# Combining a head pair's attention branches one unit later, with one more result tile

## The chip, the cores and the metric

The kernel runs on one core of a Trainium2 chip. The metric is the device time of one execution in microseconds, the median of several runs. A profiled execution gives, beside its own time, a span (first to last instruction), each engine's instructions with their times, and the clock that was granted to TensorE.

## The reference, cut to what matters

The program is a two-layer decoder trunk over 1024 tokens of width 1024. Layer 0 mixes tokens with a gated MLP and with attention of 8 heads of 64; layer 1 has a gated linear attention; each layer ends in a gated MLP with a convolution. The change lies in the attention of layer 0:

```python
B_BRANCHES = ((128, 1), (512, 4), (2048, 16))
...
    outs, lses = [], []
    for window, dilation in B_BRANCHES:
        o_r, l_r = dilated_branch(qh, kh, vh, window, dilation)
        outs.append(o_r)
        lses.append(l_r)
    wts = jax.nn.softmax(jnp.stack(lses), axis=0)
    o = jnp.einsum('rbhs,rbhsc->bhsc', wts, jnp.stack(outs))
```

Each branch is a causal attention in a sliding window over tokens of a certain stride, normalised by itself; the branches' results are then weighted by a softmax over their log-denominators. The kernel has two passes for this: one over neighbouring tokens (called n) and one over tokens with stride 4 (called d), whose mask and counts take in the third branch.

## The kernel before, in words

The engines are written T (TensorE, PE in the profile), V (VectorE, DVE), A (ScalarE, ACT), G (GpSimd, POOL) and Q (the DMA queue of SyncE, SP). The 1024 tokens are 8 tiles of 128, the 8 heads are 4 pairs.

For each pair p, `project(p)` (L741) goes over the 8 token tiles. `projected(n)` (L752) multiplies the normalised tokens by the pair's weights into a PSUM tile pj (24 matmuls of 384 columns; the tag has two banks), squares q and k on ScalarE, takes 1/rms on GpSimd (rq, L767), and writes the scaled q and k to qn on VectorE (L768). That last instruction is the last reader of pj and frees its bank. ScalarE copies v to vN, and a DMA stores it to vd (L764). Then q and k are split in two parts, turned by TensorE (tq, tk) and copied to qT and kT.

Behind each tile stands a `unit` (L715), the attention of one token tile for both heads s: score matmuls (sc, L706), the mask and the row minimum on VectorE (sm, L711), the exponential on ScalarE (L712), transposes on TensorE (pP, L726), a copy pT back to SBUF (L729 on ScalarE for odd units, L731 on VectorE for even ones), and the products with v into po (L734). Four units share one PSUM tile po and one result tile ot (L738): 128 columns of result, and per head the negated maximum and the denominator, 132 x 4 floats per partition. ScalarE copies po to ot behind each fourth unit (L808).

When the 8 units are through, `dilated(p)` (L816) runs 8 more units over tokens of stride 4. Their order of rows is another, so their two result tiles go out to DRAM (od, L829) and come back in token order as `on` (L867), one for each half of the tokens.

`combine(p, g)` (L833) and `combined` (L845) weigh the two results of half g: cM, the minimum of the two negated maxima (L838, VectorE), the differences (L841), an exponential on ScalarE (L842), the weighted denominators and their reciprocal (L849 to L852), the two products with the results (L855, one on GpSimd and one on VectorE), the sum (L857), and a DMA to bcat (L858), from which the output projection reads much later (L1204).

Combine of pair p is called from inside `project(p + 1)`, through `then` (L809): half 0 behind unit n = 3, half 1 behind unit n = 4. The last pair is combined from `u_proj` instead. Up to five ot tiles exist at once (L738).

The order in which an engine issues its instructions is not that of the code. The framework plans it: it runs a simulated timeline, and each engine takes from what is ready there the instruction that comes first in the code. Waits on semaphores are then put where data need them. In this plan the projections run ahead of the units; TensorE projects pair p + 1 while the units of pair p are still going on, and pair p + 2 while those of p + 1 are. `keep_in_program_order` around cM (L838) pins it behind the instruction that was traced just before it on VectorE; with half 0 that is the last score reduction (L711) of unit 3, an odd unit. An engine's issue is strictly in its planned order, so that an instruction which waits holds all behind it.

Of the kernel before, what the change touches and what calls it, by code (L numbers as in the profile page):

```python
# [9 lines left out]
F32 = mybir.dt.float32  # L10
# [9 lines left out]
P = 128  # L20
# [22 lines left out]
def f32(ap):  # L43
    return ap.bitcast(F32)
# [6 lines left out]
def rows(t, n):  # L51
    return t[n * P : (n + 1) * P, :]
# [3 lines left out]
def trunk(ctx: ExitStack, tc: tile.TileContext, a, out):  # L56
# [41 lines left out]
    def split(dst, src, hi=None, lo=None):  # L98

        (hi or A.copy)(dst[0], src)  # L100
        (lo or V.tensor_sub)(dst[1], src, f32(dst[0]))  # L101
# [35 lines left out]
    def inv_rms(ssq, cols, n, name, r=None):  # L137
        if r is None:
            r = small.tile([P, cols], F32, tag="rs%d" % cols, name=name)
        G.tensor_scalar(r, ssq, 1.0 / n, EPS, op0=ALU.mult, op1=ALU.add)  # L140
        G.tensor_tensor(r, r, mhalf[:, :cols], op=ALU.pow)
        return r
# [36 lines left out]
    def tok(n, k):  # L179
        return [hq[k % 2][n // 4][:, i, k // 2, (n % 4) * P : (n % 4 + 1) * P] for i in range(2)]  # L180

    def mm_tok(ps, lhs, rhs, nk):

        for k in range(nk):
            L, R = lhs(k), rhs(k)
            for i in range(2):
                for o, sl in ps:
                    for ii, jj in PASSES:
                        if ii == i:
                            T.matmul(o, L[i], R[jj][:, sl], start=(k == 0 and (ii, jj) == PASSES[0]),  # L190
                                     stop=(k == nk - 1 and (ii, jj) == PASSES[-1]))
# [422 lines left out]
    def load_qkv(p, wx, between=None):  # L614

        ws = []
        for kp in range(4):
            raw = load_raw(a["w_qkv"][p, kp], f"wq{p}{kp}r", 768)
            if between:
                between(kp)  # L620
            for i in range(2):
                k = 2 * kp + i
                src, gain = raw[:, i * 384 : i * 384 + 384], g0[:, k : k + 1]
                if p % 2 or k >= 4:
                    ws.append(parts_of(src, f"wq{p}{kp}_{i}", gain=gain))
                else:
                    w = wx.tile([P, 2, 384], F32R, tag="wx", name=f"wx{p}{k}")
                    ws.append([w[:, j, :] for j in range(2)])
                    scaled(ws[-1], src, gain)
        return ws  # L630
# [63 lines left out]
    def attention(ps, at, av, pq, pq0, par0, wx, wq0, gqk, masks, rest, gm_open):  # L694
# [3 lines left out]
        def by4(t):  # L698

            return t.rearrange("p s (m r) -> p s r m", r=4)  # L700
# [34 lines left out]
                             start=(j == 0), stop=(j == nj - 1))  # L735

        def outputs(name):
            return (at.tile([P, 4, 132], F32, tag="ot", name="ot" + name, bufs=5),  # L738
                    ps.tile([P, 4, P], F32, tag="po", name="po" + name))

        def project(p, ws=None, then=None, early=None):  # L741


            ws = ws or load_qkv(p, wx)
            pool = pq if p % 2 else pq0
            qR = pool.tile([P, 2, S], F32R, tag="qR", bufs=1, name=f"qR{p}")
            kT = pool.tile([P, 4, S], F32R, tag="kT", bufs=1, name=f"kT{p}")
            vd = dram.tile([S, P], F32, name=f"vd{p}")
            vN, os, qns = [], [], []
            heads = lambda t: t.rearrange("p (h c) -> p h c", c=64)  # L750

            def projected(n):  # L752

                pj = ps.tile([P, 512], F32, tag="pt" if early and n in (1, 3) else "pj", name=f"pj{p}{n}")
                mm_tok([(pj[:, :384], slice(0, 384))], lambda k: tok(n, k),
                       lambda k: ws[k], KD)
                qn = pq.tile([P, 256], F32, tag="qn", bufs=5, name=f"qn{p}{n}")
                rn = r0[:, n : n + 1]
                A.activation(qn, pj[:, :256], AF.Square, scale=rn)
                vN.append(pq.tile([P, P], F32, tag="vN", bufs=6, name=f"vN{p}{n}"))  # L760
                got = A.mul(vN[n], pj[:, 256:384], rn)
                if early:
                    early(n, got)
                Q.dma_start(rows(vd, n), vN[n])  # L764
                ssq = small.tile([P, 4], F32, tag="ss4", name=f"ss{p}{n}")
                V.reduce_sum(ssq, heads(qn), axis=AX.X)
                r = inv_rms(ssq, 4, 64, f"rq{p}{n}")  # L767
                V.scalar_tensor_tensor(heads(qn), heads(pj[:, :256]), rn, r[:, :, None].to_broadcast([P, 4, 64]),  # L768
                                       op0=ALU.mult, op1=ALU.mult)
                both = qn.rearrange("p (a s c) -> p a s c", a=2, s=2)  # L770
                G.tensor_tensor(both, both, gqk[:, :, None, :].to_broadcast([P, 2, 2, 64]), op=ALU.mult)
                qns.append(qn)

            lead = 3 if early else 0
            for n in range(lead):
                projected(n)
            for n in range(NT):
                if n + lead < NT:
                    projected(n + lead)
                qn = qns[n]  # L780
                qs = pq.tile([P, 2, P], F32R, tag="qs", bufs=2, name=f"qs{p}{n}")
                ks = pq.tile([P, 4, P], F32R, tag="ks", bufs=2, name=f"ks{p}{n}")
                split([qs[:, :, :64], qs[:, :, 64:]], heads(qn[:, :P]), hi=G.tensor_copy)
                kk = ks.rearrange("p (h i) (x c) -> p h i x c", i=2, x=2)
                split([kk[:, :, i] for i in range(2)], heads(qn[:, P:])[:, :, None, :].to_broadcast([P, 2, 2, 64]),
                      hi=G.tensor_copy)
                tq = ps.tile([P, 2, P], F32R, tag="tq", name=f"tq{p}{n}")
                for j in range(2):
                    T.transpose(tq[:, j, :], qs[:, j, :], identr)
                ts_ = slice(n * P, n * P + P)  # L790
                qT = pq.tile([P, 2, P], F32R, tag="qT", bufs=3, name=f"qT{p}{n}")
                A.copy(qT, f32(tq))
                four = lambda t: t.rearrange("p s (r m) -> p s r m", r=4)[:, :, :, 32 * n : 32 * n + 32]
                G.tensor_copy(four(qR), by4(f32(qT)))
                tk = ps.tile([P, 4, P], F32R, tag="tq", name=f"tk{p}{n}")
                for j in range(4):
                    T.transpose(tk[:, j, :], ks[:, j, :], identr)
                (V.tensor_copy if n % 2 else A.copy)(four(kT), by4(f32(tk)))

                if n % 4 == 0:  # L800
                    ot, po = outputs(f"{p}n{n}")
                    os.append(ot)
                m0 = max(n - 1, 0)
                unit(p, f"{p}n{n}", n % 4, ot, po, lambda s, qT=qT: qT[:, s],
                     lambda s, i: kT[:, 2 * s + i, :].rearrange("p (r m) -> p r m", r=4)[:, :, 32 * m0 : 32 * n + 32],
                     vN[m0 : n + 1], mband, lambda t: t.rearrange("p (m r) -> p r m", r=4))
                if n % 4 == 3:
                    A.copy(ot[:, :, :P], po)  # L808
                if then and n in (3, 4):  # L809
                    then(n - 3)  # L810
            v4 = av.tile([P, 4, 2, P], F32, tag="v4", name=f"v4{p}", bufs=1)
            for b in range(2):
                Q.dma_start(v4[:, :, b, :], vd.rearrange("(b m r) c -> b m r c", b=2, r=4)[b])
            return os, qR, kT, v4
# [30 lines left out]
        def combined(p, g, os, den, e):  # L845
# [12 lines left out]
            Q.dma_start(bcat[g].rearrange("(n p) c -> p n c", p=P)[:, :, p * P : p * P + P], o0)  # L858

        made = project(0, wq0, early=rest)  # L860
        for p in range(PAIRS):
            os, *qkv = made
            od = dilated(p, *qkv)
            ons = []
            for g in range(2):
                on = at.tile([P, 4, 132], F32, tag="on", name=f"on{p}{g}", bufs=2)
                Q.dma_start(on, od.rearrange("(n p) c -> p n c", p=P)[:, 4 * g : 4 * g + 4, :])  # L867
                ons.append(on)

            def weights(g):  # L870
                return combine(p, g, [os[g], ons[g]])

            def then(g):
                weights(g)()

            if p + 1 < PAIRS:
                made = project(p + 1, then=then)
            if p + 2 == PAIRS:
                par0.close()
                gm = gm_open()  # L880
# [465 lines left out]
```

## Time and profile before

| | us |
|---|---|
| median of 3 runs | 2161.59 |
| lowest and highest run | 2159.29, 2165.72 |
| the profiled execution, its time | 2167.37 |
| its span | 2165.6 |
| TensorE busy | 2134.3 |
| VectorE busy | 1530.0 |
| ScalarE busy | 1035.0 |
| GpSimd busy | 491.0 |

The span is made of stages: the attention of layer 0 with its projections takes the first 350 us or so, its gated MLP and output projection overlap with the end of it, and the rest are the two convolution MLPs and layer 1. A row of the timeline gives start and duration in us, the engine, the line of the code, the operation, output<-inputs and the number of merged instructions; in brackets stands how long the engine was idle before it, and what ended this. In tile names the buffer numbers are left out, but the pair stays: ot1n is the near result of pair 1, sm2n a score tile of pair 2. The granted clock is a share of full speed.

### The profile page before, as it was taken

Reading aid. Unit: us, or ns where it says so; the run is one execution under the profiler, and the core shown is the slowest. Engines: PE = TensorE matmul, PEld = TensorE weight load, DVE = VectorE, ACT = ScalarE, POOL = GpSimd, SP = SyncE. Lnnn points to the kernel's source line nnn. Section 1 sums busy time; section 2 is a strip of 40 time slices with the busy share of each in tenths; the row PEclk is TensorE's granted clock in tenths of the full one; section 3 lists DMA queues with packets and bytes.
Section 4 is the critical chain, followed back from the end, with each engine's and each line's share of the span. In section 5 each row is a group of like instructions: output and inputs, shape, how many; then the busy total and the mean of one; then the engine's idle time right before and its main releaser. Section 6 shows DMA issues by size and latency. Waiting matters only on the chain.

```text
span 2165.6 us, 29712 instructions
## 1 busy us (share of the span) xinstructions
PE 2134.3 (99%) x10444; PEld 1808.8 (84%) x10444; DVE 1530.0 (71%) x2451; ACT 1035.0 (48%) x1998; POOL 491.0 (23%) x521
## 2 busy tenths in 40 slices
PE   8999999999999999999999999999999999999999
PEld 7999988888888888878889888888788888888887
DVE  7566655577888878755577777667788878885554
ACT  7445555354444445444454455534544444444443
POOL 6444411012433424000010011110233425320000
PEclk9999999999999999999999999999999999999999
DMA  7022312664444444675554223386554444457664
GB/s 271 25 72 67 106 40 78 228 220 170 161 168 153 151 160 161 225 255 190 197 195 132 69 98 101 122 293 228 185 166 160 157 151 154 164 180 277 217 216 166
DMA packets 159413, 353.70 MB, mean 163 GB/s; under 512 B 17392, under 2 KB 54256, under 8 KB 158880
## 3 DMA queue, kind: packets, MB, share of 16 engines
q1 hardware_dynamic: 159264, 351.81, 47.6%
q8 instruction: 82, 1.34, 0.2%
q14 instruction: 67, 0.55, 0.1%
HBM read 243.15 MB, written 108.59 MB: 162 GB/s over the span
## 4 chain that ended last, share of the span: by engine, by line
PE 88%; DMA 5%; DVE 3%; ACT 3%; issue 1%; SPq 0%; POOL 0%; ACTq 0%; DVEq 0%
PE puB L290 11%; PE pgB L290 11%; PE pv L190 6%; PE pj L190 6%; PE pgC L290 6%; PE puC L290 6%; PE pdB L397 5%; PE pdC L397 5%; PE po L190 5%; PE pdO L397 4%; PE puA L290 3%; PE pgA L290 3%; PE pdP L397 2%; PE pdQ L397 2%; PE pu L190 2%; PE pBq L1051 2%
## 5 line engine op out<-in xcount | busy, mean ns | idle before, releaser
L101 DVE TENSOR_TENSOR da<-ar,da 128x512 fp32r<-128x512 f32 x154 | 106.3, 690 | 153.4 <-ACT da L100 153.2
L100 ACT CAST da<-ar 128x512 fp32r<-128x512 f32 x154 | 95.9, 623 | 206.9 <-PE pdC L397 97.5
L190 PE MATMUL po<-wo,hq 128*128 128x512 f32 x768 | 184.9, 395 | 2.0 <-ACT hq L100 1.8
L190 PEld LDWEIGHTS po<-wo,hq 128*128 128x128 f32 x768 | 141.3, 188 | 32.9 <-ACT hq L100 2.5
L190 PE MATMUL pv<-wv,hq 128*128 128x512 f32 (+2 forms) x768 | 140.7, 340 | 1.6 <-DVE b L1083 1.6
L397 PE MATMUL pdB<-dw,da 128*128 128x512 f32 x528 | 135.5, 391 | 1.5 <-ACT dw L100 0.8
L397 PE MATMUL pdC<-dw,da 128*128 128x512 f32 x528 | 135.1, 390 | 0.0
L190 PEld LDWEIGHTS pv<-wv,hq 128*128 128x128 f32 x768 | 118.7, 189 | 16.4 <-DVE b L1083 2.1
L397 PEld LDWEIGHTS pdB<-dw,da 128*128 128x128 f32 x528 | 98.7, 188 | 22.9 <-ACT dw L100 1.2
L256 POOL TENSOR_TENSOR S1g<-rg 128x512 f32<-128x512 f32 x20 | 30.7, 1536 | 383.0 <-DMA wsd<-D 325.8
L190 PE MATMUL pj<-wq,hq 128*128 128x384 f32 x576 | 114.7, 348 | 2.7 <-DVE qn L768 2.7
L397 PEld LDWEIGHTS pdC<-dw,da 128*128 128x128 f32 x528 | 99.0, 188 | 20.5
L101 DVE TENSOR_TENSOR dw<-wr,dw 128x512 fp32r<-128x512 f32 x154 | 105.8, 687 | 13.1 <-ACT dw L100 12.9
L140 POOL TENSOR_SCALAR rn<-ssq 128x1 f32<-128x1 f32 x24 | 8.1, 339 | 453.2 <-ACT h L148 246.0
L190 PEld LDWEIGHTS pj<-wq,hq 128*128 128x128 f32 x576 | 103.4, 195 | 3.0 <-DVE qn L768 3.0
L100 ACT CAST dw<-wr 128x512 fp32r<-128x512 f32 x154 | 95.0, 617 | 17.3 <-DMA wr<-in_w_dn 9.5
L397 PE MATMUL pdO<-dw,da 128*128 128x512 f32 x396 | 102.2, 389 | 0.2 <-DVE dw L101 0.2
L397 PEld LDWEIGHTS pdO<-dw,da 128*128 128x128 f32 x396 | 74.3, 188 | 16.0 <-DVE dw L101 0.6
L319 DVE SCALAR_TENSOR_TENSOR t<-g,cw,t 128x1022 f32<-128x1022 f32 x44 | 76.6, 1742 | 0.1
L318 DVE SCALAR_TENSOR_TENSOR t<-g,cw,t 128x1023 f32<-128x1023 f32 x44 | 60.2, 1367 | 16.2 <-ACT t L317 16.2
L303 DVE TENSOR_TENSOR g<-g,s1g 128x512 f32<-128x512 f32 x22 | 16.2, 737 | 77.2 <-ACT s1g L302 77.2
L320 ACT ACTIVATE t<-t 128x1024 f32<-128x1024 f32 x44 | 46.7, 1061 | 32.2 <-DVE t L319 32.2
(1080 smaller groups left out, 5448.3 us busy)
## 6 DMA issues: line engine op xcount, KB each, us to landing
ar<-actd SPq DMA_DIRECT2D x70, 512.0 KB, 3.6
rd<-in_w_down SPq DMA_DIRECT2D x44, 512.0 KB, 3.6
wsd<-D SPq DMA_DIRECT2D x88, 256.0 KB, 2.4
rg<-in_w_gate SPq DMA_DIRECT2D x42, 512.0 KB, 3.5
ru<-in_w_up SPq DMA_DIRECT2D x42, 512.0 KB, 4.5
wr<-wsd SPq DMA_DIRECT2D x40, 512.0 KB, 4.5
actd<-t SPq DMA_DIRECT2D x66, 256.0 KB, 2.1
wr<-in_w_dn SPq DMA_DIRECT2D x30, 512.0 KB, 4.8
```

What stands on the lines that cost most here:

```text
L100: (hi or A.copy)(dst[0], src)
L101: (lo or V.tensor_sub)(dst[1], src, f32(dst[0]))
L140: G.tensor_scalar(r, ssq, 1.0 / n, EPS, op0=ALU.mult, op1=ALU.add)
L190: T.matmul(o, L[i], R[jj][:, sl], start=(k == 0 and (ii, jj) == PASSES[0]), stop=(k == nk - 1 and (ii, jj) == PASSES[-1]))
L256: G.tensor_tensor(sums[name], x, y, op=op)
L290: T.matmul(o, L[ii][:, j * P : j * P + P], right[p][:, jj, j, :], skip_group_check=more, start=(not more and j == 0 and (ii, jj) == PASSES ...
L303: V.tensor_add(C22, C22, s1)
L318: V.scalar_tensor_tensor(t[:, 1:], g[:, : S - 1], w(1), t[:, 1:], op0=ALU.mult, op1=ALU.add)
L319: V.scalar_tensor_tensor(t[:, 2:], g[:, : S - 2], w(0), t[:, 2:], op0=ALU.mult, op1=ALU.add)
L320: A.activation(t, t, AF.Silu)
L397: T.matmul(o, L[ii][:, t * P : t * P + P], R[jj], skip_group_check=more, start=start and not more and (ii, jj) == PASSES[0], stop=stop and ...
L1051: T.matmul(o, L[ii][:, j * P : j * P + P], right[p][:, jj, j, :], skip_group_check=more, start=(not more and j == 0 and (ii, jj) == PASSES ...
```

## The change

The two calls of `then` move from behind units 3 and 4 to behind units 4 and 5, and the tag ot has six tiles instead of five.

```diff
         def outputs(name):
-            return (at.tile([P, 4, 132], F32, tag="ot", name="ot" + name, bufs=5),
+            return (at.tile([P, 4, 132], F32, tag="ot", name="ot" + name, bufs=6),
                     ps.tile([P, 4, P], F32, tag="po", name="po" + name))
...
                 if n % 4 == 3:
                     A.copy(ot[:, :, :P], po)
-                if then and n in (3, 4):
-                    then(n - 3)
+                if then and n in (4, 5):
+                    then(n - 4)
```

At the point of the call for half 0, the last instruction traced on VectorE is now unit 4's copy pT (L731, an even unit); for half 1 it is unit 5's last score reduction (L711).

## The prediction

> **What bounds the kernel now.** I read the page first, its busy times and its chain.
>
> ```profile
> span 2165.6 us, 29712 instructions
> PE 2134.3 (99%) x10444; PEld 1808.8 (84%) x10444; DVE 1530.0 (71%) x2451; ACT 1035.0 (48%) x1998; POOL 491.0 (23%) x521
> PE 88%; DMA 5%; DVE 3%; ACT 3%; issue 1%; SPq 0%; POOL 0%; ACTq 0%; DVEq 0%
> ```
>
> TensorE is busy for all but 31 us, so a change pays only where TensorE stands still or runs at a lower clock. The change lies between the head pairs, in the first 280 us. There the chain in order of time (start, us, what) leaves TensorE at the end of each pair's dilated branch:
>
> ```profile
> 118.93 3.25 DMA od<-ot0d
> ...
> 122.31 2.80 DMA on<-od
> ...
> 125.14 0.04 DVE cM L838
> ...
> 125.25 0.62 DVE sm1n L711
> ...
> 125.87 0.40 DVE qn L768
> ...
> 126.32 5.05 PE pj L190 x19
> ```
>
> The dilated result goes out to DRAM (L829) and comes back as on (L867). VectorE stands at cM (L838), the first instruction of combine(0, 0), until it lands. Behind cM, in VectorE's own order, is qn (L768), which frees the PSUM bank for the next projection. The timeline (start, us, engine, line, what, idle before and its releaser) gives the size at the first boundary:
>
> ```profile
> 109.49 1.37 POOL L141 TENSOR_TENSOR rq<-rq,mhalf 128x4 f32<-128x4 f32 x1
> 122.87 0.09 DVE L711 DVE_READ_ACCUMULATOR2_ANT ot1n<- 128x1 f32 x1
> 123.78 0.40 PE L726 MATMUL pP1n<-ident,sm1n 128*128 128x128 f32 x2
> 125.14 0.17 DVE L838 TENSOR_TENSOR cM<-ot0n,on 128x8 f32<-128x8 f32 x1 [2.18 <-DMA on<-od]
> 126.32 3.82 PE L190 MATMUL pj<-wx,hq 128*128 128x384 f32 x12 [2.13 <-DVE qn L768]
> 133.81 2.24 PE L190 MATMUL pj<-wx,hq 128*128 128x384 f32 x12
> ```
>
> VectorE is free at 122.96 and waits 2.18 us; TensorE ends its transposes at 124.18 and waits 2.13 us. The second boundary shows the same, and the third has the wait on VectorE alone:
>
> ```profile
> 193.75 0.17 DVE L838 TENSOR_TENSOR cM<-ot1n,on 128x8 f32<-128x8 f32 x1 [2.41 <-DMA on<-od]
> 195.29 5.17 PE L190 MATMUL pj<-wq,hq 128*128 128x384 f32 x15 [2.74 <-DVE qn L768]
> 266.35 0.17 DVE L838 TENSOR_TENSOR cM<-ot2n,on 128x8 f32<-128x8 f32 x1 [2.87 <-DMA on<-od]
> ```
>
> At the third there is no further pair to project; TensorE has the next stage's pv matmuls, and the windows (us, PE busy, other engines' busy, clock, DMA) have it at 63.73 of 64.00 us:
>
> ```profile
> 257.00:321.00 64.00, 63.73 (x368) 54.72 (x366) 35.82 (x106) 32.28 (x80) 12.30 (x21) 1.00 0.20 60
> ```
>
> There is a second loss. The same twelve pj matmuls take 3.82 us at 126.32 and 2.24 at 133.81. Windows of half a microsecond (us, PE busy, granted clock, DMA share, GB/s) say why:
>
> ```profile
> 51.00:51.50 0.50, 0.50 (x5) 0.55 0.84 252
> 57.50:58.00 0.50, 0.50 (x4) 0.62 0.00 0
> ...
> 126.00:126.50 0.50, 0.18 (x1) 0.64 0.96 261
> 129.50:130.00 0.50, 0.50 (x5) 0.94 0.03 10
> ...
> 194.50:195.00 0.50, 0.00 (x0) 0.50 0.14 27
> 201.00:201.50 0.50, 0.50 (x5) 0.76 0.00 0
> ```
>
> The granted clock is 0.50 from about 126.1 to 129.5 and from about 194.5 to 201.1, each time from inside a gap of TensorE. Matmuls at half the clock lose half the time: (129.5 - 126.32) x 0.5 = 1.6 us and (201.1 - 195.29) x 0.5 = 2.9 us. A third half-clock stretch, 51.2 to 57.9, lies elsewhere.
>
> **The change part by part.**
>
> Moving then(0) from behind unit 3 to behind unit 4. cM is pinned behind the VectorE instruction traced just before it. Today that is unit 3's last score reduction (L711), long done at 122.96. After the change it is unit 4's copy of the transposed scores (L731, even units copy on VectorE):
>
> ```profile
> 132.47 0.69 DVE L731 COPY pT1n<-pP1n 128x512 f32<-128x512 f32 x1 [0.83 <-PE pP1n L726]
> 136.71 0.48 DVE L768 SCALAR_TENSOR_TENSOR qn<-pj,r,rq 128x256 f32<-128x256 f32 x1
> 139.66 2.24 PE L190 MATMUL pj<-wx,hq 128*128 128x384 f32 x12
> 142.30 0.48 DVE L768 SCALAR_TENSOR_TENSOR qn<-pj,r,rq 128x256 f32<-128x256 f32 x1 [1.18 <-POOL rq L141]
> 145.42 1.90 PE L190 MATMUL pj<-wx,hq 128*128 128x384 f32 x10
> ```
>
> That copy comes 7.3 us after on landed (125.14); even if all behind the boundary moves up by 3.7 us, on has been there for over 3 us. So the wait goes and none of its kind replaces it. VectorE then runs the score reduction and qn 2.18 us earlier: qn ends at 125.77 + 0.49 - 2.18 = 124.08, before TensorE ends its transposes at 124.18. Its other input, rq, was last written at 110.9. Nothing is late next: the idle of **2.13 us** goes whole, and by the same working **2.74 us** at the second boundary. The third gives 0: the reading with TensorE at 63.73 of 64.00 is the nearest row, the upper bound is the 2.87 us that VectorE waits.
>
> The half clock. With the gap gone, the stretch before 126.1 holds matmuls throughout. I take it that the clock then stays, and 1.6 + 2.9 = **4.5 us** go too; the lower bound is 0.
>
> [...]
>
> The combine later, both in a row. One combine costs, by groups of the lines view between 113 and 215 us (count | busy, mean ns | idle before):
>
> ```profile
> L855 DVE TENSOR_TENSOR on<-on,cE 128x512 f32<-128x512 f32 x4 | 4.0, 996 | 0.1
> L855 POOL TENSOR_TENSOR ot0n<-ot0n,cE 128x512 f32<-128x512 f32 x2 | 2.6, 1298 | 0.7 <-DVE cE L852 0.7
> L857 DVE TENSOR_TENSOR ot1n<-ot1n,on 128x512 f32<-128x512 f32 x2 | 1.8, 910 | 0.1
> L850 DVE TENSOR_TENSOR cD<-cD 128x8 f32<-128x8 f32 x4 | 1.7, 427 | 0.1
> L851 DVE RECIPROCAL cD<-cD 128x8 f32<-128x8 f32 x4 | 0.8, 203 | 0.1
> L849 DVE TENSOR_TENSOR cD<-cE,on 128x8 f32<-128x8 f32 x4 | 0.6, 162 | 0.0
> ```
>
> On VectorE: 1.00 + 0.91 + 0.43 + 0.20 and six small ones (L838, L841, L849, L852) at 0.16, together 3.5 us; on GpSimd 1.3; on ScalarE one small exponential. Today combine(0, 0) lies before 132.4, combine(0, 1) behind cM at 133.07. After it both lie between unit 4's copy and unit 6, where VectorE has room:
>
> ```profile
> 132.40:143.70 11.30, 11.30 (x80) 11.26 (x78) 7.67 (x23) 4.42 (x13) 7.07 (x10) 1.00 0.21 60
> ```
>
> 7.67 + 3.5 = 11.2 of 11.30 us on VectorE, 7.07 + 1.3 = 8.4 on GpSimd: it fits, but narrowly. Queued behind are the two qn (136.71 and 142.30) on which TensorE's next projections wait; they end 139.66 - 137.19 = 2.47 us and 145.42 - 142.78 = 2.64 us before they are needed. That slack is the cover; I take the cost at 0. Without cover the first qn can be late by the whole first combine, its wait for the exponential (0.6) and GpSimd's multiply: 3.5 + 0.6 + 1.3 = 5.4 us, that is 2.9 past the slack.
>
> The output DMA (L858) of the first half moves back by one unit on SP's queue. Behind it are the stores of v (L764), read again only by the dilated units that start at 158; cost 0, since the last reader of bcat is the output projection after 368. Nothing else moves on SP or POOL's queue.
>
> The sixth tile. Today unit 4's tile is written at 122.87 with no wait, while both tiles of the pair before are still unread: it sits in the slot of a dilated tile that had gone out. A further slot adds no instruction; cost 0. It moves the tiles behind it in SBUF by 2112 bytes per partition; I see no wait that hangs on this, and take 0.
>
> The sum against the profiled execution, 2167.37 us (span 2165.6 and 1.8 around it): 2167.37 - 2.13 - 2.74 - 4.5 = 2158.0. After these stages TensorE is the bound, so the gain should reach the end. The median of the runs is 2161.59, 5.8 lower than the profiled one. Whether a gap of 2 us halves the clock must depend on where it falls in the stretches of some 3.3 us, which differs from run to run; for the median I take the idle whole and three quarters of the half-clock term, 3.4: 2161.59 - 4.87 - 3.4 = **2153.3 us**.
>
> **The rivals.**
>
> *The half clock has another cause and stays.* For it: the stretch from 51.2 to 57.9 begins without a gap of 2 us; the longest wait of TensorE before it is
>
> ```profile
> 49.57 0.74 PE L706 MATMUL sc0n<-kT,qT 128*128 128x256 f32 x4 [0.90 <-ACT kT L798]
> ```
>
> 0.90 us, in small score and transpose work like that before 126. Against: between 113 and 126 the same kind of work ran at full clock until the gap. It gives 2161.59 - 4.87 = 2156.7.
>
> *The gain is swallowed*, because the planner, which orders each engine by its own simulated times, puts other work into VectorE's freed time ahead of qn, or because cM still waits. Against: qn is the oldest work there, and on landed 7.3 us before. It gives 2161.6.
>
> *Slower: the two combines in a row hold up qn.* The place is VectorE between unit 4's copy and unit 6; it decides once more than 2.47 us stand ahead of the first qn that do not today. At the bound of 5.4 TensorE gets a new gap of 2.9 us, as long as that of 2.74 which cost 2.9 in clock: 5.8 per qn. With one qn per boundary that is 2 x 5.8 - 8.3 = +3.3, 2164.9; with both, where VectorE never catches up in its 11.3 us, 4 x 5.8 - 8.3 = +14.9, 2176.5. For it: only 0.1 us of VectorE is left over. Against: most of combine(0, 1) stands ahead of that qn already today without harm, and qn waits for GpSimd's rq, not VectorE, at 142.30.
>
> **How the numbers follow.** Forecast 0.62, half clock stays 0.10, swallowed 0.08, slower 0.20. What a measurement of this kernel can tell from no change is about 0.3%, 6.5 us: below 2155.1 or above 2168.1. Of the forecast's 0.62, 0.50 lies below 2155.1 (its own range is 2149 to 2158, the clock term between nothing and whole, and a microsecond of chance). Same: 0.12 + 0.10 + 0.08 + 0.04 of the slower case with one qn = 0.34. Slower: 0.16. The range from 2148 to 2168 takes in the whole sum with the clock term, the second and third case and the slower case with one qn; the 0.16 above it is left out.
>
> **What would show it.** Right: no wait of cM for on, no idle of pj for qn near 124 and 190, and a clock of 1.00 through both boundaries. Wrong: idle of TensorE before pj for qn one or two projections later, with VectorE in L855 or L857 or GpSimd's rq behind its multiply; or a clock of 0.50 there with no gap.

## The result and the profile after

The changed kernel takes 2154.18 us in the median of six runs (2153.44 to 2155.70), beside 2163.99 us for the kernel before on the same chip (six runs, 2159.29 to 2165.92): a ratio of 0.9961, 95% interval 0.9950 to 0.9972. The medians differ by 9.8 us; the ratio, which isn't that of the two medians, makes it 8.4 us (6.1 to 10.8), 0.39%. The forecast was 2153.3. The profiled execution took 2153.94 us.

The page after: the span, the busy times, and the shares of the chain that ended last.

```profile
span 2152.2 us, 29720 instructions
PE 2125.0 (99%) x10444; PEld 1801.6 (84%) x10444; DVE 1528.2 (71%) x2451; ACT 1034.8 (48%) x1998; POOL 490.5 (23%) x521
PE 91%; DVE 3%; DMA 2%; ACT 2%; issue 1%; SPq 0%; POOL 0%; DVEq 0%; ACTq 0%
```

The span is 13.4 us shorter and TensorE's busy time 9.3 us: most of what went was not idle, but matmuls that took longer than they had to (some of them in a stretch that has nothing to do with the change, below). The DMA's share of the chain fell from 5% to 2%.

The waits of TensorE between 100 and 300 us (who waited for whom: us in total, times, longest), all that is left of them:

```profile
PE po2d L734 <- DVE pT2d L731: 0.8, 1, 0.8
PE po1d L734 <- ACT kT L798: 0.3, 1, 0.3
```

The wait of pj for qn isn't there. The timeline after at the first boundary (start, us, engine, line, what, idle before and its releaser):

```profile
120.81 0.47 DVE L768 SCALAR_TENSOR_TENSOR qn<-pj,r,rq 128x256 f32<-128x256 f32 x1
121.34 2.35 PE L190 MATMUL pj<-wx,hq 128*128 128x384 f32 x12
126.01 0.69 DVE L731 COPY pT1n<-pP1n 128x512 f32<-128x512 f32 x1 [1.54 <-PE pP1n L726]
126.62 0.15 DVE L838 TENSOR_TENSOR cM<-ot0n,on 128x8 f32<-128x8 f32 x1
127.75 0.16 DVE L838 TENSOR_TENSOR cM<-ot0n,on 128x8 f32<-128x8 f32 x1
130.29 0.48 DVE L768 SCALAR_TENSOR_TENSOR qn<-pj,r,rq 128x256 f32<-128x256 f32 x1
131.29 1.83 DVE L855 TENSOR_TENSOR on<-on,cE 128x512 f32<-128x512 f32 x2
133.05 2.23 DVE L857 TENSOR_TENSOR ot0n<-ot0n,on 128x512 f32<-128x512 f32 x2
137.31 0.48 DVE L768 SCALAR_TENSOR_TENSOR qn<-pj,r,rq 128x256 f32<-128x256 f32 x1 [1.18 <-POOL rq L141]
```

cM stands behind unit 4's copy (L731) and no longer waits for on: the transfer of on was issued at 120.30 and such a transfer took 2.7 to 3.1 us here, so that it had landed by 123.4, 3.2 us ahead of cM. The qn runs at 120.81, and the twelve pj matmuls behind it begin with no gap and take 2.35 us where they took 3.82. The same qn ran at 125.77 before. Of these 4.96 us, 2.58 had been gained by 100 us and have nothing to do with the change (below). Matched matmul by matmul, the lead over before was 6.5 us behind the first boundary and 12.3 behind the second. So the boundaries brought 3.9 and 5.7 us, and the third nothing.

The windows of ten microseconds (us, PE busy, other engines' busy, then granted clock, DMA share, GB/s), of after:

```profile
50.00:60.00 10.00, 9.68 (x73) 9.41 (x74) 6.03 (x18) 5.85 (x18) 4.74 (x10) 1.00 0.21 66
120.00:130.00 10.00, 10.00 (x72) 9.99 (x71) 7.61 (x31) 5.08 (x17) 5.05 (x10) 1.00 0.40 101
190.00:200.00 10.00, 10.00 (x70) 10.00 (x70) 9.05 (x30) 4.69 (x14) 7.07 (x8) 1.00 0.12 35
```

and of before:

```profile
50.00:60.00 10.00, 9.69 (x52) 9.44 (x50) 5.02 (x15) 3.60 (x13) 3.77 (x7) 0.66 0.16 48
120.00:130.00 10.00, 7.87 (x54) 7.63 (x53) 6.70 (x23) 4.77 (x17) 3.70 (x6) 0.83 0.44 114
190.00:200.00 10.00, 7.26 (x40) 7.03 (x39) 7.05 (x20) 3.10 (x11) 4.72 (x7) 0.72 0.32 89
```

TensorE is busy through both boundaries at full clock: 72 matmuls in ten microseconds for 54, and 70 for 40. The window from 50 to 60 is a trap in the comparison. There too before ran at 0.66 and after at 1.00. But up to 100 us the two kernels issue the same matmuls in the same order, and the stretch comes with the move and without: 0.66 or 0.83 stands there in seven of the fourteen profiles of this study, in all four of kernels without the move and in three of the ten with it. That the move has no part in it is argued from the equal order; one profile of each kernel doesn't show it. The stretch cost the profiled execution before 3.0 us: it was 0.45 us ahead of after at 46 us and 2.54 behind at 58. So the 13.4 us between the two profiled executions are 3.0 there, 9.6 at the two boundaries, and 0.8 in small differences elsewhere.

### The profile page after: what moved, and what is told of

It reads as the page before. It is cut to its first block, busy times and chain, and to the rows that moved or that the text cites. A ratio compares the mean times of both kernels' runs of the same rounds, so it can differ in the third digit from the quotient of the medians.

```text
span 2152.2 us, 29720 instructions
## 1 busy us (share of the span) xinstructions
PE 2125.0 (99%) x10444; PEld 1801.6 (84%) x10444; DVE 1528.2 (71%) x2451; ACT 1034.8 (48%) x1998; POOL 490.5 (23%) x521
## 4 chain that ended last, share of the span: by engine, by line
PE 91%; DVE 3%; DMA 2%; ACT 2%; issue 1%; SPq 0%; POOL 0%; DVEq 0%; ACTq 0%
PE puB L290 11%; PE pgB L290 11%; PE po L190 7%; PE pv L190 6%; PE pj L190 6%; PE pgC L290 6%; PE puC L290 6%; PE pdB L397 5%; PE pdC L397 5%; PE pdO L397 4%; PE puA L290 3%; PE pgA L290 3%; PE pdP L397 2%; PE pdQ L397 2%; PE pu L190 2%; PE pBq L1051 2%
## 5 line engine op out<-in xcount | busy, mean ns | idle before, releaser
L190 PE MATMUL pj<-wq,hq 128*128 128x384 f32 x576 | 110.2, 339 | 0.0
L319 DVE SCALAR_TENSOR_TENSOR t<-g,cw,t 128x1022 f32<-128x1022 f32 x44 | 76.6, 1742 | 0.1
```

The lines of the kernel that those rows point to most:

```text
L319: V.scalar_tensor_tensor(t[:, 2:], g[:, : S - 2], w(0), t[:, 2:], op0=ALU.mult, op1=ALU.add)
```

## The experiments

**The sixth tile alone.** The places of before, with six result tiles:

```diff
-            return (at.tile([P, 4, 132], F32, tag="ot", name="ot" + name, bufs=5),
+            return (at.tile([P, 4, 132], F32, tag="ot", name="ot" + name, bufs=6),
```

> The kernel before with six ot tiles, the two calls of then left behind units 3 and 4. Theory (cM's wait for on holds qn, and that leaves TensorE idle and then at half clock): the wait stays, about 2.2 us on VectorE at the first two boundaries, and the time is that of before, 2164 (2160 to 2167), ratio 0.999 to 1.001. Rival (the sixth tile frees something): the time of the changed kernel, about 2154.

Measured: 2166.26 us (ten runs), ratio to before 1.0013 (1.0003 to 1.0022). The wait of VectorE for on between 100 and 300 us:

```profile
DVE cM L838 <- DMA on<-od: 7.2, 3, 2.8
```

The timeline of this kernel where TensorE pays for it:

```profile
126.47 1.97 PE L190 MATMUL pj<-wx,hq 128*128 128x384 f32 x5 [2.00 <-DVE qn L768]
195.03 4.91 PE L190 MATMUL pj<-wq,hq 128*128 128x384 f32 x19 [2.29 <-DVE qn L768]
264.35 3.24 PE L190 MATMUL pv<-wv,hq 128*128 128x512 f32 x13 [2.31 <-DVE qn L768]
```

And its windows at the three places:

```profile
120.00:130.00 10.00, 8.00 (x54) 7.76 (x55) 6.81 (x23) 5.06 (x17) 3.71 (x7) 0.83 0.45 118
190.00:200.00 10.00, 7.71 (x49) 7.47 (x47) 7.26 (x20) 3.30 (x12) 4.98 (x8) 0.83 0.33 92
264.00:268.00 4.00, 3.65 (x17) 3.03 (x18) 3.90 (x14) 1.99 (x7) 3.05 (x7) 1.00 0.13 38
```

All three waits of cM stay, and with them the gaps, and at the first two boundaries the half clock. This plan lets TensorE stand still at the third boundary too, for 2.31 us, which is about what this kernel is slower than before. So one wait of VectorE can or can't reach TensorE according to what the plan has put beside it: the 2.87 us at the third boundary of the kernel before left TensorE busy for 63.73 of the 64.00 us around it.

**The move alone.** Behind units 4 and 5, with five tiles:

```diff
-                if then and n in (3, 4):
-                    then(n - 3)
+                if then and n in (4, 5):
+                    then(n - 4)
```

> The calls of then moved behind units 4 and 5, with five ot tiles as before. Theory: a dilated tile's slot is free when unit 4 needs one, so nothing waits for it and the time is that of the changed kernel, 2154 (2152 to 2157). Rival (without the sixth tile unit 4's first write waits for a slot): TensorE idle before unit 4's work, 2160 or more.

Measured: 2153.83 us (four runs), ratio 0.9956 (0.9939 to 0.9973), no wait of pj for qn, clock 1.00 at both boundaries. The sixth tile isn't needed; the move is the whole change.

**The wait alone.** In the code everything stands at the places of before, but on is loaded from the input x, so that nothing waits for a round trip. This leaves the second branch out of the result.

```diff
-                Q.dma_start(on, od.rearrange("(n p) c -> p n c", p=P)[:, 4 * g : 4 * g + 4, :])
+                Q.dma_start(on, a["x"].rearrange("(n p) c -> p n c", p=P)[:, 4 * g : 4 * g + 4, :132])
```

> The kernel before, calls behind units 3 and 4, but on is loaded from the input x instead of from od, so it never waits for the dilated result; the second branch is thereby left out of the result (its stores to od still run). Theory: the wait of cM goes without moving the combine, and with it the idle time and the half clock: 2154 to 2157. Rival (it is the place of the combine in VectorE's order, or two combines close together, that pays): still about 2164.

Measured: 2155.20 us (four runs), ratio 0.9959 (0.9944 to 0.9974). Its timeline at the first boundary, cM and the first qn behind it:

```profile
121.53 0.16 DVE L838 TENSOR_TENSOR cM<-ot0n,on 128x8 f32<-128x8 f32 x1
124.68 0.47 DVE L768 SCALAR_TENSOR_TENSOR qn<-pj,r,rq 128x256 f32<-128x256 f32 x1
```

Its windows:

```profile
50.00:60.00 10.00, 9.69 (x49) 9.30 (x50) 5.73 (x16) 4.08 (x14) 4.09 (x8) 0.66 0.20 67
120.00:130.00 10.00, 9.88 (x76) 9.50 (x75) 9.58 (x35) 6.46 (x23) 4.42 (x8) 1.00 0.27 78
190.00:200.00 10.00, 10.00 (x72) 10.00 (x72) 8.86 (x27) 3.97 (x11) 6.55 (x9) 1.00 0.33 93
```

The plan, which sees the shorter way, orders some instructions otherwise, but cM still stands ahead of qn, and waits for nothing. The whole loss at the boundaries is gone, clock included. So it was the wait, not the place of combine's work. The half clock between 50 and 60 is there although the waits for on are gone, so that it is another matter.

**Later still, and half 0 alone.** First both halves one unit further on, behind units 5 and 6; then both behind unit 4, so that only half 0 moves. Both have six tiles.

```diff
-                if then and n in (4, 5):
-                    then(n - 4)
+                if then and n in (5, 6):
+                    then(n - 5)
```

> Six tiles, the calls moved one unit further, behind units 5 and 6. Theory: on has long landed behind unit 4 already, so nothing more is to be had: within 2 us of the changed kernel, 2152 to 2156. Rival (each unit of delay gains by spreading VectorE's work): 2150 or less; second rival (late combines run into the dilated units): 2158 or more.

```diff
-                if then and n in (4, 5):
-                    then(n - 4)
+                if then and n == 4:
+                    then(0)
+                    then(1)
```

> Six tiles; half 0 moved behind unit 4, half 1 left behind unit 4, where it was. Theory: only half 0 waited for on, so this alone gives the whole gain: 2154 (2152 to 2157). Rival (moving half 1 gives part of it): 2158 or more.

Measured: 2155.21 us (four runs), ratio 0.9960 (0.9945 to 0.9975), and 2156.31 us (five runs), ratio 0.9960 (0.9942 to 0.9977). Both have no wait of pj for qn and a clock of 1.00 at both boundaries; neither can be told from the change itself. Once on has landed before cM's turn, a later place brings nothing more, and the half that waited is half 0.

**More work in combine.** The change, with four further additions of 128x512 on VectorE in each combine, to find out what the cover is worth:

```diff
+            for _ in range(4):
+                V.tensor_add(o1, o1, o1)
```

> The changed kernel with four more additions of 128x512 at the end of each combine (into on, which nothing reads any more), some 2.8 to 4 us more on VectorE for each half. It asks how much cover the changed place has. By the prediction's count only 0.1 us of VectorE is left between unit 4's copy and unit 6, so qn of the next projections is held up past its slack of some 2.5 us: TensorE idle before pj, at the first two boundaries 2 us or more each, 2160 or more. Rival (the slack in the plan is larger than that count, since VectorE's waits there are not work): within 2 us of the changed kernel, 2152 to 2156.

Measured: 2160.79 us (ten runs), ratio 0.9982 (0.9971 to 0.9993), 6.6 us over the change by the medians and 4.5 by the ratios, whose intervals just touch. One addition took 0.68 us, so each combine is 2.7 us longer, the two of a boundary 5.4. What its TensorE waited for between 100 and 300 us, of 0.3 us or more:

```profile
PE pj L190 <- DVE qn L768: 1.8, 4, 0.5
```

Its timeline, the longest of these gaps and one further on:

```profile
141.67 2.38 PE L190 MATMUL pj<-wx,hq 128*128 128x384 f32 x12 [0.52 <-DVE qn L768]
373.94 0.69 PE L442 MATMUL pc<-ident,mx 128*128 128x128 f32 x2 [1.75 <-DVE hq L101]
```

And its windows there:

```profile
360.00:370.00 10.00, 10.00 (x48) 8.31 (x47) 10.00 (x18) 5.26 (x9) 0.00 (x0) 1.00 0.64 209
370.00:380.00 10.00, 7.29 (x26) 5.57 (x25) 5.87 (x10) 3.06 (x6) 0.00 (x0) 0.66 0.78 265
```

At the boundaries the 5.4 us make four short gaps, 1.8 us in all, and no half clock. The larger part is lost at another place: the last pair's combine is called from `u_proj`, its extra work keeps VectorE busy without a break from 360 to 370, the casts hq behind it come late, TensorE waits 1.75 us at 373.94 (0.20 at the same place in the change) and then runs at half the clock to 380, which costs at most (380 - 373.94) x 0.5 = 3.0 us. In the profiled execution that makes 1.8 + 1.55 + 3.0 = 6.4 us. Not every run pays the half clock: the three with a mean clock of 0.999 took 2156.5 to 2157.4 us, the seven with 0.997 or 0.998 2159.1 to 2162.8. So the time came out above 2160, as the theory had it, but for another reason: the theory's gaps of 2 us at each boundary didn't come.

**A longer way.** The kernel before, with a second hop through DRAM on the way of on:

```diff
+            oh = dram.tile([S, 132], F32, name=f"oh{p}")
+            Q.dma_start(oh, od)
+            od = oh
```

> The kernel before with a second DRAM hop on the way of on (od to oh to on), places and tiles as before: on lands about 2.8 us later still. The plan, which sees the longer way, now puts cM behind both qn. Theory (the loss comes from cM standing ahead of qn in VectorE's order, not from the length of the way): no wait of pj for qn at the first two boundaries although on comes later, 2154 to 2157. Rival (the way of on itself sets the time): 2164 + 2 x 2.8 = about 2169.

Measured: 2164.95 us (eleven runs), ratio to before 1.0011 (1.0002 to 1.0020). Neither theory: it isn't fast, and not as slow as a longer way at the old place would be. Its timeline around the first boundary, with the rows of TensorE that waited for 1.5 us or more:

```profile
123.15 0.48 DVE L768 SCALAR_TENSOR_TENSOR qn<-pj,r,rq 128x256 f32<-128x256 f32 x1
124.61 0.48 DVE L768 SCALAR_TENSOR_TENSOR qn<-pj,r,rq 128x256 f32<-128x256 f32 x1 [0.19 <-ACT vN L761]
130.85 0.17 DVE L838 TENSOR_TENSOR cM<-ot0n,on 128x8 f32<-128x8 f32 x1 [5.56 <-DMA on<-oh]
134.07 0.68 DVE L731 COPY pT1n<-pP1n 128x512 f32<-128x512 f32 x1
134.80 1.10 PE L734 MATMUL po1n<-vN,pT1n 128*128 128x64 f32 x8 [1.92 <-DVE pT1n L731]
202.92 1.10 PE L734 MATMUL po2n<-vN,pT2n 128*128 128x64 f32 x8 [1.66 <-DVE pT2n L731]
274.96 1.21 PE L726 MATMUL pP3n<-ident,sm3n 128*128 128x128 f32 x4 [1.97 <-ACT sm3n L712]
```

Its windows at the three gaps:

```profile
130.00:140.00 10.00, 7.08 (x44) 6.18 (x43) 8.33 (x30) 4.65 (x14) 4.60 (x6) 1.00 0.32 93
200.00:210.00 10.00, 7.33 (x45) 6.44 (x45) 9.07 (x27) 4.10 (x13) 6.01 (x8) 1.00 0.20 60
270.00:280.00 10.00, 8.02 (x37) 6.38 (x36) 7.58 (x25) 3.79 (x12) 3.62 (x3) 0.83 0.09 28
```

The plan did what was expected of it and put both qn ahead of cM. But on came later still, cM held VectorE for 5.56 us, and what now stood behind it was the copy pT, for which TensorE waits just as it had for qn. At the third gap it was a score reduction, by way of ScalarE. The theory was right about these two qn (a later one still kept TensorE waiting 0.84 us at 139 and 0.85 at 207) and wrong to stop there: every instruction behind the waiting one counts.

**A gap without a DMA.** Five kernels were meant to make a gap at the first two boundaries by work on VectorE ahead of the seventh qn, to see which length halves the clock. They add reductions into a small tile `late` to the changed kernel. The second of them, with one reduction of 8 x 128 elements, is shown; the first reduces half as much and halves two small tiles beside it, and the tiles of the later stages lie as in the second, 32 bytes per partition further on than in the change.

```diff
+                if p in (1, 2) and n == 6:
+                    late = small.tile([P, 8], F32, tag="late", bufs=1, name=f"late{p}")
+                    V.reduce_sum(late, vN[n][:, None, :].to_broadcast([P, 8, P]), axis=AX.X)
+                    V.scalar_tensor_tensor(late[:, :1], late[:, :1], 0.0, rn, op0=ALU.mult, op1=ALU.add)
+                    rn = late[:, :1]
```

> The changed kernel, with an extra sum of 4 x 128 values on VectorE (and a one-column instruction) that qn of the seventh token tile must wait for, in pairs 1 and 2 only: it makes qn late by a dose of its own, with no DMA and no combine in it. With the copy kT that the plan now puts ahead, qn comes about 1.3 us later and TensorE's gap is about 1.1 us at each of the two boundaries. Theory (a late qn is all that the wait did; a gap of about 2 us halves the clock, a shorter one need not): the time of the changed kernel plus 2 x 1.1 = 2156.4 (2155 to 2159), clock 1.00 at the boundaries. Rival (any gap there halves the clock): 2160 or more.

> The same with a sum of 8 x 128 values: qn comes about 2.4 us later, TensorE's gap is about 2.1 us at both boundaries, as in the kernel before, with no wait for on. Theory: both terms come back, 2154.2 + 4.2 of idle and 2 to 6 of half clock, 2160 to 2165, clock 0.50 for some 3 us or more after each gap. Rival (the half clock in the kernel before had another cause): 2158.4, clock 1.00.

Measured: 2174.50 us (seven runs), ratio 1.0041 (1.0027 to 1.0054), and 2173.85 us (six runs), ratio 1.0048 (1.0033 to 1.0062). Both miss. The gaps weren't made: the waits of TensorE in the second kernel, between 100 and 300 us, have

```profile
PE pj L190 <- DVE qn L773: 1.4, 2, 0.7
```

and the clock is 1.00. Yet both lose 17 to 19 us against the change, by the ratios. The next three have one, two and three reductions of 8 x 128 into a `late` of 64 bytes; they were to find these microseconds, and to make longer gaps.

> The kernel of e10, instruction for instruction in the same order on every engine; its extra small tile is 64 instead of 32 bytes per partition, so that the tiles behind it keep their place modulo 64 bytes. Theory (e10 lost its time to the addresses: in its feed-forward stages twelve 512-wide matmuls with T as moving operand take 2.80 us from start to start, against 2.72 after): 2154.2 + 1.4 us of idle before pj = about 2156, the FFN windows with 443 matmuls per 100 us as after, not 435. Rival (the extra VectorE work or its order costs it): about 2174, as e10.

> As e11 with the reduction twice, so that qn comes 1.2 us later than in e11: an idle of TensorE before pj of about 1.9 us at the first two boundaries with no DMA in it. Theory (a gap of this length is what halves the clock): clock 0.50 behind each gap, 2154.2 + 2 x 1.9 + 1.6 + 2.9 = about 2162. Rival (the half clock has a cause other than the gap, such as the DMA or the phase of the stage): clock 1.00 and 2154.2 + 3.8 = 2158.

> As e12 with the reduction three times: a gap of about 3.1 us at each of the two boundaries. Theory: clock 0.50 behind each gap, 2154.2 + 6.2 + 4.5 = about 2165. Rival: clock 1.00 and about 2160.4.

Measured: 2168.41 us (eight runs), ratio 1.0030 (1.0020 to 1.0041); 2166.02 us (eleven), 1.0018 (1.0010 to 1.0027); 2168.98 us (seven), 1.0032 (1.0021 to 1.0044). The first lies between its theory and its rival, the other two above both. Again no gap between 100 and 300 us was longer than 0.8 us. The plan gave TensorE other work meanwhile, which it hadn't done for on in the kernel before (gaps of 2.13 and 2.74 us). So the length of gap that halves the clock was not measured in this way.

The lost time lies elsewhere. A window over the first convolution MLP, of the change:

```profile
500.00:900.00 400.00, 399.32 (x1762) 330.45 (x1761) 332.73 (x361) 187.10 (x299) 137.05 (x75) 1.00 0.49 161
```

The same of the kernel with 32 bytes more and one reduction:

```profile
500.00:900.00 400.00, 399.32 (x1730) 324.33 (x1729) 331.92 (x353) 184.66 (x293) 140.22 (x77) 1.00 0.47 156
```

And of that with 64 bytes more and one reduction:

```profile
500.00:900.00 400.00, 399.32 (x1740) 326.19 (x1739) 331.50 (x354) 184.03 (x293) 140.77 (x77) 1.00 0.47 156
```

TensorE is busy all the time at full clock, and does 1762, 1730 and 1740 matmuls in 400 us. Each matmul takes longer. The timelines show by how much. Of the change:

```profile
599.64 1.98 PE L290 MATMUL pgB<-T,wg6p 128*128 128x512 f32 x8
601.45 0.62 PE L290 MATMUL puB<-hq,wu6p 128*128 128x512 f32 x2
```

Of the kernel with 32 bytes more:

```profile
603.09 2.97 PE L290 MATMUL pgB<-T,wg6p 128*128 128x512 f32 x12
605.89 0.63 PE L290 MATMUL puB<-hq,wu6p 128*128 128x512 f32 x2
```

Of that with 64 bytes more:

```profile
603.67 2.93 PE L290 MATMUL pgB<-T,wg6p 128*128 128x512 f32 x12
606.44 0.63 PE L290 MATMUL puB<-hq,wu6p 128*128 128x512 f32 x2
```

From start to start one matmul with T as an operand takes 1.81 / 8 = 226 ns, 2.80 / 12 = 233 ns and 2.77 / 12 = 231 ns. The second and the third kernel issue the same instructions in the same order on every engine and differ only in where the tiles behind `late` lie in SBUF, T among them. So the place alone, 32 bytes, makes a difference: that is shown. The other three bear it out, for their counts in the same window go by the place and not by the work: 1730 with 32 bytes and half the reduction, 1740 and 1742 with 64 bytes and two or three reductions. That the remaining loss of the third kernel comes from its 64 bytes is argued, since no kernel moves the tiles without adding work: the kernels with further additions and with two hops do other work at the boundaries, move no tile of this stage, and have 1763 and 1767 matmuls in the same window. The bill, an estimate from these counts: two such MLPs of 400 us lose 2 x 400 x (1762 - 1740) / 1762 = 10 us with 64 bytes and 14.5 us with 32; with 1.4 us of gaps that is 11.4 and 15.9 of the 15 and 19 us that the ratios show against the change. The remaining 3 us weren't followed up.

## Why the prediction was right, point by point

- **The wait goes, and none takes its place: right.** cM stands behind unit 4's copy, on landed 3.2 us ahead of it (the prediction had over 3), and qn comes at 120.81, ahead of TensorE's need. The move alone and the kernel without the round trip have the gain, the sixth tile alone hasn't.
- **The idle of 2.13 and 2.74 us goes whole: right.** The waits of TensorE between 100 and 300 us hold no pj after.
- **The half clock goes with it: right; its share in the median can't be told from the noise.** The clock is 1.00 through both boundaries in the change, in the move alone, and in the kernel without the round trip. For the profiled execution idle and the whole term give 4.87 + 4.5 = 9.4 us, and the boundaries show 3.9 + 5.7 = 9.6. For the median the prediction took three quarters of the 4.5, since the term would differ from run to run with the place of the gap in stretches of some 3.3 us. The three quarters were its author's estimate, and no run shows that the place decides. What the runs show is that the clock differs: in 26 further runs of the kernel before, the four with a mean clock of 0.999 took 2157.95 to 2161.45 us, the six with 0.995 or 0.996 2163.13 to 2169.46. The gain was put at 8.3 us; it is 9.8 by the medians and 8.4 by the ratio (6.1 to 10.8).
- **That the forecast is only 0.9 us off is partly luck:** the kernel before moved too, from 2161.59 us in three runs to 2163.99 in six.
- **The sum against the profiled execution, 2158.0, was 4.1 us too high.** It left the stretch from 51.2 to 57.9 in, rightly, since the change doesn't touch it; the profiled execution after happened not to have it. That is 3.0 of the 4.1 us.
- **The third boundary 0, the sixth tile 0, the store on SP's queue 0: right for the change,** as far as the move alone and the waits after show. That no wait hangs on the sixth tile doesn't hold at the old place: alone it made the plan let TensorE stand still 2.31 us at the third boundary (ratio 1.0013).
- **The cover for combine: right that it costs nothing, too pessimistic about what is left.** The prediction read 11.2 of 11.30 us from busy times. With 5.4 us more on VectorE the gaps are 0.5 us at most. The rows after say why: the plan put both sets of multiplications and additions (131.29 to 135.28) behind the qn of 130.29, and the next qn still waits 1.18 us for GpSimd. A sum of busy times in a window says nothing of the order in it.
- **The rivals.** "The half clock has another cause and stays" falls by the clock of 1.00 at both boundaries in the kernel without the round trip; with the sixth tile alone, where the wait stays, the windows around the gaps of 2.00 and 2.29 us have 0.83. "Swallowed" falls: the plan put nothing ahead of qn. "Slower" needed two combines ahead of one qn, which the plan didn't do.

## What to carry to other kernels

Where a plan orders an engine by simulated times, look for an instruction that waits for a DMA round trip: what stands behind it on its engine waits with it (here cM stood 2.18 us, and TensorE 2.13 for the qn behind it). Move it behind work that surely comes later than the landing, and read what stands behind it there, for that will wait next if the guess is wrong again. Price a gap of TensorE like these two at about twice its length, as an estimate from what they cost with the half clock behind them (2.13 us of idle cost 3.9, and 2.74 cost 5.7); and when a small tile is added, compare the matmuls per microsecond in stages that have nothing to do with it (here 1762 in 400 us became 1730).

## What the runs showed of the hardware that was not expected

- **A gap of about 2 us may halve TensorE's clock, and may not.** Between 100 and 400 us, clock below 1.00 came behind gaps of 1.75 us (more work in combine, with 0.96 us of idle 2.5 us ahead of it), 1.97 (two hops), 2.00 and 2.29 (the sixth tile alone), 2.13 and 2.74 us (before); it stayed 1.00 behind 1.66 and 1.92 (two hops) and 2.31 us (the sixth tile alone). No gap of up to 0.85 us between 100 and 300 us brought it down. So these gaps show no sharp length between 1.66 and 2.31 us.
- **The clock's changes lie on a grid in the profiles read for it.** Eight profiles were read in windows of half a microsecond from 40 to 400 us, and four of them have changes; the times are worked out from the clock of the windows. Before: 51.05, 57.88, 126.14, 129.56, 194.41 and 201.24 us. With more work in combine: 52.23, 55.65, 373.08 and 379.91. With two hops: 52.79, 56.20, 274.65 and 278.06. With three reductions: 50.94 and 57.77. Within each profile they lie whole multiples of 3.41 us apart (3.413 fits all of them to 0.03 us), and each half-clock stretch is 3.41 or 6.83 us long. Before, the clock fell 1.95 and 1.86 us into the gaps of 2.13 and 2.74 us; with two hops 1.66 us into that of 1.97, and with more work 0.89 us into that of 1.75. Why it fell in these and not in others, the runs don't show, nor whether the place of a gap on the grid has a part in it.
- **The place of a tile in SBUF changes the pace of matmuls.** A matmul took 226 ns in the change, 231 and 233 ns with the tiles of that stage 64 and 32 bytes further on; 32 bytes alone, the order being equal, make 1740 matmuls in 400 us into 1730. Which places are fast, and by what rule, the runs don't say.
